# Seven products of half blocks for eleven pairs of feature tiles, and a squared relu on ScalarE alone

## The chip, the cores and the metric

One core of a Trainium2 chip runs the whole program. The metric is device time in microseconds. A matrix product runs on TensorE (PE in the profile, its weight loads PEld), elementwise work on VectorE (DVE), ScalarE (ACT) and GpSimd (POOL); SyncE (SP) issues the transfers from DRAM.

## The reference

The program computes two blocks of a sequence model in a row, on 512 tokens of width 1024, in float32. The first has a gated linear recurrence, a pooling branch and an attention to a memory, the second a spatial gating, a gated linear attention and a feed-forward part. The change lies in the feed-forward part, at the end of the second block:

```python
h = layer_norm(DEEPNORM_ALPHA * h + m @ w_out[l], ln1_g[l], ln1_b[l])     # 512 x 1024
f = jnp.square(jax.nn.relu(h @ w_ff1[l])) @ w_ff2[l]                      # 1024 -> 4096 -> 1024
h = layer_norm(DEEPNORM_ALPHA * h + f, ln2_g[l], ln2_b[l])
```

## The kernel before, in words

**Products.** Every float32 operand is split into a high part, rounded to the format fp32r, and a low part, the rest: a copy by ScalarE (`split`, L558) and a subtraction by VectorE. A product of two 128-row blocks is then three matmuls into the same accumulator (`mm3`, L575): high x high, high x low, low x high. Activations lie feature-major: a page (`pg`, 64 of them, 128 x 512) holds 128 features of all 512 tokens. PSUM has eight banks of 128 x 512.

**Weights.** They come in chunks of 512 KB, in one fixed order (`chunks`, L599). `load_to` has SP load a chunk into one of four raw buffers (tag wr); `split_to` splits it into one of four slots for the high parts (tag wh) and one of four for the low parts (wl), at an offset of columns that `shift` gives for some chunks (16 for the key projection of the memory). Chunks named in `paged` are split into pages instead. `chunk` hands out the next one.

**The stage.** After the layer norm `ln1`, `h1h` and `h1l` hold the split activations in eight pages each, and `ha` the unsplit ones. The first product (1024 -> 4096) makes 32 tiles of 128 features. Tiles 0 to 3 are one group (L1924 to L1955), with all tokens of half HA (0 to 255) first and then HB, because the norm of HB is still being computed. Tiles 4 to 31 are units (`unit_fm`, L1984): one chunk, 8 k-blocks times three matmuls of 512 columns into one bank, then ScalarE's relu out of PSUM and VectorE's product of relu and PSUM, into a page of `ff`. The second product (4096 -> 1024) then uses all eight banks; its tokens stand on the partitions, so the residual needs `ha` in tokens: `to_tokens` (L1964) transposes three of the four token tiles on TensorE, as a side lane that runs between the units, and the fourth is added in PSUM by a product of `ha` with the scaled identity `idl` (L2013).

**Order.** Nothing runs as it is called. `Recorder` (L168) records every operation; `order` (L324) lays out the whole program with a list schedule over PE, ACT, DVE, POOL and SP: each operation has a modelled cost, a priority (the latest start, worked back from the end) and the tiles it needs a free buffer for. The best of six rounds is issued, so each engine has one fixed queue. All instructions are issued from one line (L500), so the profile is read by the names of the tiles: ps is PSUM, wh and wl the weight slots, wr the raw weights, pg the pages, ct the constants.

Of the kernel before, what the change touches and what calls it, by code (L numbers as in the profile page):

```python
# [8 lines left out]
F32 = mybir.dt.float32  # L9
F32R = mybir.dt.float32r  # L10
U32 = mybir.dt.uint32
ACTF = mybir.ActivationFunctionType
ALU = mybir.AluOpType
# [7 lines left out]
ISQ = 128.0 ** -0.5  # L21

SLOT = 1088


VECS = [
# [141 lines left out]
class Recorder:  # L168
# [335 lines left out]
ORDER1 = [(w[:-1], int(w[-1])) for w in (  # L504
    "o0 o1 o2 o3 q0 k0 qc0 km0 km1 km2 km3 q1 k1 vm0 vm1 vm2 vm3 qc1 q2 k2 "
    "q3 qc3 qc2 k3 u0 u1 u2 u3 zb0 zb1 zb2 zb3 za0 za1 za2 za3 zc0 zc1 zc2 zc3").split()]
ORDER2 = [(w[:-1], int(w[-1])) for w in (
    "au0 au1 au2 au3 au4 au5 au6 au7 q0 k0 q1 r0 k1 q2 k2 q3 k3 r1 r2 r3 "
    "r4 r5 r6 r7 ga0 ga1 ga2 ga5 ga3 ga4 ga6 ga7 gb0 gb1 gb2 gb3 gb4 gb5 gb6 gb7").split()]
# [3 lines left out]
def tile_two_blocks(ctx, tc, wa, wb, xT, memT, vec, cst, rows, poolw, wst, wg2, out):  # L513
    ctx.enter_context(tc.manual_schedule())
    rec = Recorder(tc.nc)
    V, A, G, PE, SP = [Engine_(rec, e) for e in ("DVE", "ACT", "POOL", "PE", "SP")]

    per = ctx.enter_context(tc.tile_pool(name="per", bufs=1))
    sb = ctx.enter_context(tc.tile_pool(name="sb", bufs=1))
# [4 lines left out]
    def name(p):  # L524
        cnt[0] += 1
        return f"{p}{cnt[0]}"

    def pg(n=T, dt=F32):
        return rec.tile(sb, [128, n], dt, tag="pg", name=name("pg"), bufs=NPG)

    def big(n=2 * T):
        return rec.tile(sb, [128, n], F32, tag="big", name=name("big"), bufs=4)

    def bank():
        return rec.tile(psum, [128, T], F32, tag="ps", bufs=8, name=name("ps"))
# [7 lines left out]
    def tt(eng, out, a, b, op):  # L543
        eng.tensor_tensor(out=out, in0=a, in1=b, op=op)
# [10 lines left out]
    def act(out, in_, func, **kw):  # L555
        A.activation(out=out, in_=in_, func=func, **kw)

    def split(hi, lo, src, scale=None, eng=None):  # L558

        if scale is None:  # L560
            act(hi, src, ACTF.Copy)
            tt(eng or V, lo, src, f(hi), ALU.subtract)
        else:
            act(hi, src, ACTF.Copy, scale=scale)
            stt(lo, src, scale, f(hi), ALU.mult, ALU.subtract)

    def split_pg(src, n=T, **kw):
        hi, lo = pg(n, F32R), pg(n, F32R)
        split(hi, lo, src, **kw)
        return hi, lo  # L570

    def mm(out, l, r, start, stop):
        PE.matmul(out=out, lhsT=l, rhs=r, start=start, stop=stop)

    def mm3(out, lh, ll, rh, rl, start, stop):  # L575
        mm(out, lh, rh, start, False)
        mm(out, lh, rl, False, False)
        mm(out, ll, rh, False, stop)
# [30 lines left out]
            nb += 1  # L609
    RAW, HL = 4, 4  # L610
    raw, wsp, paged = {}, {}, set()

    shift = {4 + i: 16 for i, w in enumerate(ORDER1) if w[0] == "km"}
    shift.update({4 + len(ORDER1) + 12 + i: 48 for i in range(8)})
    shift[4 + len(ORDER1) + 12 + 16 + len(ORDER2) + 4] = 16
    n_ld, n_sp, look = [0], [0], [2]
# [10 lines left out]
    def load_to(i):  # L627
        while n_ld[0] <= min(i, NCH - 1):
            c = n_ld[0]
            t = rec.tile(sb, [128, src[c].shape[1]], F32, tag="wr", name=f"wr{c}", bufs=RAW)  # L630
            SP.dma_start(out=t, in_=src[c])
            raw[c] = t
            n_ld[0] += 1

    def split_to(i):
        while n_sp[0] <= min(i, NCH - 1):
            c = n_sp[0]
            t = raw.pop(c)
            n = src[c].shape[1]
            if c in paged:  # L640
                h, l = Pair(), Pair()
                for i in range(2):
                    split(h.pages[i], l.pages[i], t[:, i * T:(i + 1) * T])
            else:
                o = shift.get(c, 0)
                h = rec.tile(sb, [128, SLOT], F32R, tag="wh", name=f"wh{c}", bufs=HL)[:, o:o + n]
                l = rec.tile(sb, [128, SLOT], F32R, tag="wl", name=f"wl{c}", bufs=HL)[:, o:o + n]
                split(h, l, t)
            wsp[c] = (h, l)
            n_sp[0] += 1  # L650
# [5 lines left out]
    def lane(quick=False):  # L656
        q = deque()
        lanes.append(q)
        if quick:
            fast.append(q)  # L660
        return q
# [20 lines left out]
    ci = [0]  # L682
# [8 lines left out]
    def run_ahead():  # L691
        c = ci[0] - 1 + look[0]
        while n_sp[0] <= min(c, NCH - 1):
            load_to(n_sp[0])
            split_to(n_sp[0])
            load_to(n_sp[0] - 1 + RAW)

    def unit(emit, evac=None, early=False):
        first = True
        for _ in emit(*chunk()):  # L700
            if first:
                run_ahead()
                first = False
            step(fast)
        if early and evac:
            evac()
        step(lanes)
        if not early and evac:
            evac()

    def fm(ps, ah, al, n=T):
        def emit(wh, wl):
            for k in range(8):
                s = slice(k * 128, (k + 1) * 128)
                mm3(ps[:, 0:n], wh[:, s], wl[:, s], ah[k], al[k], k == 0, k == 7)
                if k == 3:
                    yield
        return emit

    def unit_fm(ah, al, evac, n=T):  # L720
        ps = bank()
        unit(fm(ps, ah, al, n), lambda: evac(ps))

    def units_tok(ah, al, ncol, evac, k_first=False, late=False):

# [83 lines left out]
    xh, xl = [], []  # L809
    first = []  # L810
    if True:
# [14 lines left out]
        for k in range(8):  # L826
            s = slice((k % 4) * 260, (k % 4 + 1) * 260)
# [9 lines left out]
        for k in range(8):  # L837
            s = slice((k % 4) * 260, (k % 4 + 1) * 260)
            w = first[k // 4]
            h, l = split_pg(xraw[k], scale=vc("norm_g", k))  # L840
# [61 lines left out]
    for c in range(2):  # L902
        def evac(j, ps, c=c):
            s = slice(c * 256, c * 256 + 256)
            split(vh[j][:, s], vl[j][:, s], ps[:, 0:256], scale=rxc[:, j:j + 1])
            stt(gt[:, c, j, :], ps[:, 256:260], rxc[:, j:j + 1], rsm[:, 4 * c:4 * c + 4], ALU.mult, ALU.add)
# [73 lines left out]
    mh, ml = [], []  # L980
# [784 lines left out]
    ha = []  # L1765
# [34 lines left out]
    s1 = [None]  # L1800
# [18 lines left out]
    s2 = pg()  # L1819
# [22 lines left out]
    h1h = [pg(T, F32R) for _ in range(8)]  # L1842
    h1l = [pg(T, F32R) for _ in range(8)]
# [36 lines left out]
    ps = col_sum(s1[0], 4)  # L1880
# [7 lines left out]
    p = bank()  # L1888
# [35 lines left out]
    ff = [None] * 32  # L1924
    ps_f = [bank() for _ in range(4)]
    g2 = ln1(HB)
    plan = {(0, 0): "ge", (0, 1): "gG", (1, 0): "gG", (1, 1): "g", (2, 0): "gG", (2, 1): "gG", (3, 0): "gG", (3, 1): "gG"}
    for hf in (HA, HB):
        for u in range(4):
            if hf is HA:  # L1930
                W.append(chunk())
            for kk in range(2):
                k = 2 * u + kk
                for m in range(4):
                    s = slice(kk * 512 + m * 128, kk * 512 + (m + 1) * 128)
                    mm3(ps_f[m][:, hf], W[u][0][:, s], W[u][1][:, s], h1h[k][:, hf], h1l[k][:, hf], k == 0, k == 7)
                if hf is HA:
                    for c in plan[u, kk]:
                        if c == "g":
                            next(g, None)  # L1940
                        elif c == "G":
                            next(g2)
                        else:
                            evac_half(3, HB)
                    if kk == 0 and u < 3:
                        run_ahead()
                else:
                    next(g2, None)
                    if u == 3 and kk == 0:
                        run_ahead()  # L1950
        for m in range(4):
            if hf is HA:
                ff[m] = pg()
            act(ff[m][:, hf], ps_f[m][:, hf], ACTF.Relu)
            tt(V, ff[m][:, hf], ps_f[m][:, hf], ff[m][:, hf], ALU.mult)  # L1955
    W.clear()
    del s1, s2, sq, ps_f, ps_h


    idl = pg()[:, 0:128]  # L1960
    ts(idl, ident, ALPHA, None, ALU.mult)
    ht = [[pg() for _ in range(2)] for _ in range(3)]

    def to_tokens():  # L1964
        yield
        for j in range(3):
            for c in range(2):
                p = bank()
                for i in range(4):
                    PE.transpose(out=p[:, i * 128:(i + 1) * 128], in_=ha[4 * c + i][:, j * 128:(j + 1) * 128], identity=ident)  # L1970
                act(ht[j][c], p, ACTF.Copy, scale=ALPHA)
                yield

    tl = lane()
    tl.append(to_tokens())
    def evac_f(i):
        def e(ps):
            t = pg()
            act(t, ps, ACTF.Relu)
            tt(V, t, ps, t, ALU.mult)  # L1980
            ff[i] = t
        return e

    for i in range(4, 32):  # L1984
        unit_fm(h1h, h1l, evac_f(i))
    drain_side()
    del h1h, h1l
# [24 lines left out]

    for c in range(2):  # L2013
        for i in range(4):
            mm(po[3][c][:, i * 128:(i + 1) * 128], ha[4 * c + i][:, 384:512], idl, i == 0, False)
    ha.clear()
    del idl

    split_f(0)
    split_f(1)  # L2020
# [191 lines left out]
```

## Time and profile before

| | |
|---|---|
| runs, median (lowest to highest) | 1135.74 us (1134.62 to 1136.75) |
| profiled execution | 1136.61 us |
| its span, first to last instruction | 1134.7 us |
| granted TensorE clock, mean | 0.993 of 2.4 GHz |
| PE busy | 1117.9 us, 99%, 5808 matmuls |
| DVE busy | 710.1 us, 63% |
| ACT busy | 515.8 us, 45% |
| POOL busy | 183.6 us, 16% |
| chain that ended last | PE 98%, DVE 1% |

A row of the timeline gives the start and the length of a run of equal instructions, and in brackets how long the engine had been idle and what ended that. A matmul's length in the trace overlaps the next one's, so its price is read from the distance of starts. A row of the windows gives busy time and number of instructions of each engine in a stretch, the granted clock and the share and rate of the DMA.

### The profile page before, as it was taken

The numbers are of one execution on the slowest core, as the hardware profiler recorded it, in microseconds if no ns is written. First come the engines' busy times: TensorE is split into PE (matmuls) and PEld (weight loads), VectorE is DVE, ScalarE is ACT, GpSimd is POOL, SyncE is SP. The second block draws the span as 40 slices with busy tenths as digits, with TensorE's granted clock in tenths as the row PEclk, the third lists the DMA queues.
The fourth block names the chain that finished last, engine by engine and source line by source line (L and its number), as shares of the span: only waits on it lengthen the run. The fifth ranks groups of instructions, "written<-read, shape, count | busy, mean of one in ns | idle before, by whom it ended". The sixth has DMA issues, their size and how long they took to land.

```text
span 1134.7 us, 15224 instructions
## 1 busy us (share of the span) xinstructions
PE 1117.9 (99%) x5808; PEld 954.4 (84%) x5808; DVE 710.1 (63%) x1291; ACT 515.8 (45%) x868; POOL 183.6 (16%) x244
## 2 busy tenths in 40 slices
PE   8999999999999999999999999999999999999997
PEld 8888888878889999788888887888888888888885
DVE  6978887887436565568768867986333337333324
ACT  7766536444334533874565534546332326222311
POOL 5212102000101000344145560002000000000005
PEclk9999999999999999899999999999999999999999
DMA  8324222422232322222221131431223223234201
GB/s 306 113 94 168 84 75 84 142 101 97 90 111 87 103 75 75 75 95 73 75 93 57 56 112 42 144 113 37 72 83 106 93 93 111 93 120 140 75 1 74
DMA packets 33799, 108.85 MB, mean 96 GB/s; under 512 B 3888, under 2 KB 5040, under 8 KB 33728
## 3 DMA queue, kind: packets, MB, share of 16 engines
q1 hardware_dynamic: 33728, 107.90, 28.4%
q8 instruction: 45, 0.74, 0.3%
q14 instruction: 26, 0.21, 0.1%
HBM read 105.79 MB, written 2.10 MB: 95 GB/s over the span
## 4 chain that ended last, share of the span: by engine, by line
PE 98%; DVE 1%; ACT 0%; DMA 0%; issue 0%; SPq 0%
PE ps L500 98%; DVE pg L500 0%; DMA wr<-in_wb_dram 0%; ACT pg L500 0%; DVE sm L500 0%; ACT wh L500 0%; DVE wl L500 0%; SPq L500 0%; ACT bhl L500 0%
## 5 line engine op out<-in xcount | busy, mean ns | idle before, releaser
L500 PE MATMUL ps<-pg,wh 128*128 128x512 f32 (+1 forms) x1952 | 597.0, 388 | 0.0
L500 PEld LDWEIGHTS ps<-pg,wh 128*128 128x128 f32 x1952 | 361.7, 189 | 73.5 <-PE ps L500 1.0
L500 PE MATMUL ps<-pg,wl 128*128 128x512 f32 (+1 forms) x976 | 375.7, 385 | 0.0
L500 ACT ACTIVATE wh<-wr 128x1024 fp32r<-128x1024 f32 (+2 forms) x159 | 163.1, 1026 | 322.4 <-PE ps L500 291.7
L500 DVE TENSOR_TENSOR wl<-wr,wh 128x1024 fp32r<-128x1024 f32 (+1 forms) x151 | 188.8, 1252 | 161.3 <-ACT wh L500 161.0
L500 PE MATMUL ps<-pg,pg 128*128 128x512 f32 (+4 forms) x1280 | 239.4, 343 | 1.4 <-ACT pg L500 1.4
L500 PEld LDWEIGHTS ps<-pg,pg 128*128 128x128 f32 (+1 forms) x1280 | 206.0, 191 | 30.8 <-ACT pg L500 2.3
L500 PEld LDWEIGHTS ps<-pg,wl 128*128 128x128 f32 x976 | 183.8, 188 | 37.0
L500 POOL TENSOR_TENSOR pg<-pg,pg 128x128 f32<-128x128 f32 (+4 forms) x113 | 109.5, 976 | 650.2 <-ACT pg L500 466.0
L500 ACT ACTIVATE pg<-pg 128x512 fp32r<-128x512 f32 (+6 forms) x254 | 133.4, 550 | 100.4 <-DVE pg L500 91.1
L500 PE MATMUL ps<-wh,pg 128*128 128x260 f32 (+2 forms) x800 | 169.0, 307 | 5.5 <-ACT wh L500 5.5
L500 DVE TENSOR_TENSOR pg<-ps,pg 128x512 f32<-128x512 f32 (+4 forms) x153 | 95.3, 630 | 77.2 <-PE ps L500 68.3
L500 DVE TENSOR_TENSOR pg<-pg,pg 128x512 f32<-128x512 f32 (+7 forms) x207 | 122.5, 616 | 30.3 <-PE ps L500 13.9
L500 PEld LDWEIGHTS ps<-wh,pg 128*128 128x128 f32 x800 | 130.6, 191 | 12.3 <-ACT wh L500 5.5
L500 PE MATMUL ps<-wl,pg 128*128 128x260 f32 (+2 forms) x400 | 121.4, 305 | 0.0
L500 PEld LDWEIGHTS ps<-wl,pg 128*128 128x128 f32 x400 | 76.4, 191 | 3.6 <-issue 0.5
L500 DVE TENSOR_TENSOR pg<-wr,pg 128x512 fp32r<-128x512 f32 x62 | 40.8, 689 | 61.3 <-issue 41.5
L500 ACT ACTIVATE pg<-wr 128x512 fp32r<-128x512 f32 x62 | 35.4, 624 | 83.6 <-PE ps L500 75.2
L500 DVE SCALAR_TENSOR_TENSOR pg<-pg,pg 128x512 f32<-128x512 f32 (+4 forms) x76 | 54.8, 739 | 4.5 <-ACT pg L500 4.0
L500 ACT ACTIVATE pg<-ps 128x512 f32<-128x512 f32 (+5 forms) x78 | 39.7, 529 | 12.7 <-PE ps L500 12.2
L500 ACT ACTIVATE pg<-pg,vt 128x512 f32<-128x512 f32 (+3 forms) x60 | 38.9, 656 | 13.5 <-DVE pg L500 12.1
L500 DVE SCALAR_TENSOR_TENSOR pg<-pg,vt,pg 128x512 fp32r<-128x512 f32 (+4 forms) x48 | 37.5, 793 | 6.3 <-ACT pg L500 5.4
(131 smaller groups left out, 540.6 us busy)
## 6 DMA issues: line engine op xcount, KB each, us to landing
wr<-in_wa_dram SPq DMA_DIRECT2D x172, 512.0 KB, 3.4
wr<-in_wb_dram SPq DMA_DIRECT2D x10, 520.0 KB, 3.6
pg<-in_xT_dram SPq DMA_DIRECT2D x16, 256.0 KB, 4.1
pg<-in_rows_dram SPq DMA_DIRECT2D x10, 256.0 KB, 4.2
out_dram<-pg SPq DMA_DIRECT2D x8, 256.0 KB, 2.0
wr<-in_wb_dram SPq DMA_DIRECT2D x8, 130.0 KB, 4.0
pg<-in_memT_dram SPq DMA_DIRECT2D x4, 256.0 KB, 7.1
pg<-in_wst_dram SPq DMA_DIRECT2D x2, 256.0 KB, 4.4
```

Source lines behind the costliest of these rows:

```text
L500: getattr(real[o.eng], o.what)(**kw)
```

## The change

Tiles 4 to 25, eleven pairs, are computed by a scheme of seven block products (Strassen and Winograd's). A pair's weights are a 2 x 2 array of blocks: two tiles (the raw chunks a and c) by two halves of the contraction (lo: k-blocks 0 to 3, hi: 4 to 7). The activations are a 2 x 2 array too: the same two halves of k by two halves of the tokens. `pair_weights` builds four weight slots from a, c, s1 = c.lo + c.hi, s2 = s1 - a.lo, a.lo - c.lo and a.hi - s2, with VectorE and into `big` buffers or in place. `fast_operands` builds the differences of the activation blocks once, for all pairs. `pair_fast` runs the seven products, each over four k-blocks at 256 columns, into halves of four banks, and recombines them with five VectorE instructions and a copy by ScalarE. The chunks of the pairs are skipped by `split_to`. The relu's square is taken by ScalarE, in the first group and in the units left (26 to 31) too. The transposes to tokens are recorded as a whole ahead of the pairs, and the fourth token tile of `ha` is copied into two pages (`hr`).

```diff
+NFAST = 11
...
+    FF1 = 4 + len(ORDER1) + 12 + 16 + len(ORDER2) + 8
+    fast_ff = set(range(FF1 + 4, FF1 + 4 + 2 * NFAST))
...
     def split_to(i):
         while n_sp[0] <= min(i, NCH - 1):
             c = n_sp[0]
+            if c in fast_ff:
+                n_sp[0] += 1
+                continue
...
+    def pair_weights():
+        i = ci[0]
+        ci[0] += 2
+        load_to(i + 1)
+        split_to(i + 1)
+        a, c = raw.pop(i), raw.pop(i + 1)
+        lo, hi = slice(0, 512), slice(512, 1024)
+        def slot():
+            h = rec.tile(sb, [128, SLOT], F32R, tag="wh", name=name("fh"), bufs=HL)[:, 16:16 + 1024]
+            l = rec.tile(sb, [128, SLOT], F32R, tag="wl", name=name("fl"), bufs=HL)[:, 16:16 + 1024]
+            return h, l
+        def part(w, s):
+            return w[0][:, s], w[1][:, s]
+        w1 = slot()
+        split(*w1, a)
+        s1, s2 = big(768)[:, 0:512], big(768)[:, 0:512]
+        tt(V, s1, c[:, lo], c[:, hi], ALU.add)
+        tt(V, s2, s1, a[:, lo], ALU.subtract)
+        tt(V, c[:, lo], a[:, lo], c[:, lo], ALU.subtract)
+        w2 = slot()
+        split(*part(w2, lo), s2)
+        split(*part(w2, hi), s1)
+        w3 = slot()
+        split(*w3, c)
+        tt(V, a[:, hi], a[:, hi], s2, ALU.subtract)
+        w4 = slot()
+        split(*part(w4, lo), a[:, hi])
+        load_to(i + 3)
+        return w1, w2, w3, w4
+
+    def pair_fast(b, evac, w=None):
+        w1, w2, w3, w4 = w or pair_weights()
+        lo, hi = slice(0, 512), slice(512, 1024)
+        p16, p23, p7, p45 = [bank() for _ in range(4)]
+        L, R = slice(0, 256), slice(256, 512)
+        def product(o, w, s, m):
+            wh, wl = w[0][:, s], w[1][:, s]
+            for kk in range(4):
+                q = slice(kk * 128, (kk + 1) * 128)
+                mm3(o, wh[:, q], wl[:, q], b[m][0][kk], b[m][1][kk], kk == 0, kk == 3)
+        product(p16[:, L], w1, lo, 1)
+        product(p16[:, R], w2, lo, 6)
+        product(p7[:, L], w3, lo, 7)
+        product(p45[:, R], w2, hi, 5)
+        product(p23[:, L], w1, hi, 2)
+        product(p45[:, L], w3, hi, 4)
+        product(p23[:, R], w4, lo, 3)
+        c1, c2, u = pg(), pg(), big(768)
+        act(c1[:, L], p16[:, L], ACTF.Copy)
+        tt(V, u[:, L], p16[:, R], c1[:, L], ALU.add)
+        tt(V, u[:, R], p7[:, L], u[:, L], ALU.add)
+        tt(V, c1[:, R], p45[:, R], u[:, L], ALU.add)
+        tt(V, c1, p23, c1, ALU.add)
+        tt(V, c2.rearrange("p (a n) -> p a n", a=2), p45.rearrange("p (a n) -> p a n", a=2),
+           u[:, R].unsqueeze(1).to_broadcast([128, 2, 256]), ALU.add)
+        evac(c1, c2)
+
+    def fast_operands(x, xh, xl):
+        L, R = slice(0, 256), slice(256, 512)
+        b = {m: ([None] * 4, [None] * 4) for m in range(1, 8)}
+        for kk in range(4):
+            j = kk + 4
+            for m, (t, s) in {1: (kk, L), 2: (j, L), 3: (j, R)}.items():
+                b[m][0][kk], b[m][1][kk] = xh[t][:, s], xl[t][:, s]
+            t56, t74 = pg(), pg()
+            tt(V, t56[:, L], x[kk][:, R], x[kk][:, L], ALU.subtract)
+            tt(V, t56[:, R], x[j][:, R], t56[:, L], ALU.subtract)
+            tt(V, t74[:, L], x[j][:, R], x[kk][:, R], ALU.subtract)
+            tt(V, t74[:, R], x[j][:, L], t56[:, R], ALU.subtract)
+            for (ml, mr), t in (((5, 6), t56), ((7, 4), t74)):
+                h, l = split_pg(t)
+                for m, s in ((ml, L), (mr, R)):
+                    b[m][0][kk], b[m][1][kk] = h[:, s], l[:, s]
+        return b
...
                     if u == 3 and kk == 0:
-                        run_ahead()
+                        w = pair_weights()
         for m in range(4):
             if hf is HA:
                 ff[m] = pg()
             act(ff[m][:, hf], ps_f[m][:, hf], ACTF.Relu)
-            tt(V, ff[m][:, hf], ps_f[m][:, hf], ff[m][:, hf], ALU.mult)
+            act(ff[m][:, hf], ff[m][:, hf], ACTF.Square)
...
-    tl = lane()
-    tl.append(to_tokens())
+    fb = fast_operands(ha, h1h, h1l)
+    for i in range(8):
+        act(hr[i // 4][:, (i % 4) * 128:(i % 4 + 1) * 128], ha[i][:, 384:512], ACTF.Copy)
+    for _ in to_tokens():
+        pass
+    ha.clear()
+
     def evac_f(i):
         def e(ps):
             t = pg()
             act(t, ps, ACTF.Relu)
-            tt(V, t, ps, t, ALU.mult)
+            act(t, t, ACTF.Square)
             ff[i] = t
         return e
 
-    for i in range(4, 32):
+    def evac_pair(i):
+        def e(*cs):
+            for k, t in enumerate(cs):
+                act(t, t, ACTF.Relu)
+                act(t, t, ACTF.Square)
+                ff[i + k] = t
+        return e
+
+    for i in range(4, 4 + 2 * NFAST, 2):
+        pair_fast(fb, evac_pair(i), w)
+        w = None
+    fb.clear()
+    for i in range(4 + 2 * NFAST, 32):
         unit_fm(h1h, h1l, evac_f(i))
...
-            mm(po[3][c][:, i * 128:(i + 1) * 128], ha[4 * c + i][:, 384:512], idl, i == 0, False)
+            mm(po[3][c][:, i * 128:(i + 1) * 128], hr[c][:, i * 128:(i + 1) * 128], idl, i == 0, False)
```

## Rows read from the trace of the kernel before

**Rows 1.** The page's engine totals: busy us, share of the span, instructions.
```profile
PE 1117.9 (99%) x5808; PEld 954.4 (84%) x5808; DVE 710.1 (63%) x1291; ACT 515.8 (45%) x868; POOL 183.6 (16%) x244
```

**Rows 2.** The chain that ended last, in order of time: start, length, what.
```profile
785.35 340.96 PE ps L500 x1548
```

**Rows 3.** Windows: length, busy us (instructions) by engine, clock, DMA share, GB/s.
```profile
764.00:786.00 22.00, 19.11 (x146) 17.72 (x146) 17.59 (x51) 14.02 (x32) 3.94 (x5) 0.98 0.15 48
786.00:790.30 4.30, 4.30 (x27) 4.25 (x27) 3.74 (x10) 3.65 (x9) 1.47 (x2) 0.70 0.01 4
790.30:795.40 5.10, 5.10 (x45) 5.10 (x44) 0.02 (x1) 0.78 (x3) 0.73 (x1) 1.00 0.00 0
...
802.00:857.00 55.00, 55.00 (x253) 45.54 (x252) 18.27 (x20) 16.94 (x25) 0.00 (x0) 1.00 0.28 93
```

**Rows 4.** Timeline, ScalarE in two units: start, length, operation, idle before.
```profile
801.06 1.06 ACT L500 ACTIVATE wh<-wr 128x1024 fp32r<-128x1024 f32 x1 [4.63 <-PE ps L500]
...
802.02 0.58 ACT L500 ACTIVATE pg<-ps 128x512 f32<-128x512 f32 x1
...
806.50 1.06 ACT L500 ACTIVATE wh<-wr 128x1024 fp32r<-128x1024 f32 x1 [3.89 <-PE ps L500]
```

**Rows 5.** Timeline, TensorE in the key projection of the memory.
```profile
82.06 0.28 PE L500 MATMUL ps<-pg,wl 128*128 128x256 f32 x1
...
84.10 0.28 PE L500 MATMUL ps<-pg,wl 128*128 128x256 f32 x1
```

**Rows 6.** Timeline, TensorE in the out projection at half width.
```profile
734.37 0.28 PE L500 MATMUL ps<-pg,wl 128*128 128x256 f32 x1
...
735.78 0.28 PE L500 MATMUL ps<-pg,wl 128*128 128x256 f32 x1
```

**Rows 7.** Timeline, TensorE in the first feed-forward group, half HB.
```profile
789.14 6.87 PE L500 MATMUL ps<-pg,pg 128*128 128x256 f32 x56
...
795.84 0.40 PE L500 MATMUL ps<-pg,wh 128*128 128x512 f32 x1
```

**Rows 8.** Groups by form, 700 to 1000 us: count, busy us, mean ns, idle before.
```profile
L500 DVE TENSOR_TENSOR wl<-wr,wh 128x1024 fp32r<-128x1024 f32 x41 | 50.1, 1225 | 102.3 <-ACT wh L500 102.2
...
L500 DVE TENSOR_TENSOR pg<-ps,pg 128x256 f32<-128x256 f32 x16 | 6.6, 424 | 10.3 <-ACT pg L500 5.4 <-PE ps L500 4.9
...
L500 DVE TENSOR_TENSOR pg<-pg,pg 128x512 f32<-128x512 f32 x9 | 6.2, 689 | 0.3
```

**Rows 9.** Timeline, runs of equal instructions on VectorE and ScalarE.
```profile
723.98 2.36 DVE L500 TENSOR_TENSOR wl<-wr,wh 128x1024 fp32r<-128x1024 f32 x2
...
764.55 1.99 DVE L500 TENSOR_TENSOR pg<-pg,ps 128x256 f32<-128x256 f32 x5
...
954.38 3.70 DVE L500 TENSOR_TENSOR pg<-pg,pg 128x512 fp32r<-128x512 f32 x6
...
958.66 3.83 ACT L500 ACTIVATE pg<-pg 128x512 fp32r<-128x512 f32 x7
```

**Rows 10.** The page's DMA issues: count, KB each, us to landing.
```profile
wr<-in_wa_dram SPq DMA_DIRECT2D x172, 512.0 KB, 3.4
```

**Rows 11.** Timeline, four transposes to tokens between two units.
```profile
811.97 0.60 PE L500 MATMUL ps<-ct,pg 128*128 128x128 f32 x4
```

**Rows 12.** Timeline, TensorE at the first of three equal stops.
```profile
783.16 0.62 PE L500 MATMUL ps<-pg,pg 128*128 128x256 f32 x3 [0.47 <-ACT pg L500]
```

**Rows 13.** Windows behind these stops; the third last number is the granted clock.
```profile
785.00:786.00 1.00, 0.65 (x3) 0.65 (x4) 0.14 (x2) 0.97 (x3) 0.00 (x0) 0.58 0.00 0
786.00:787.00 1.00, 1.00 (x6) 1.00 (x6) 1.00 (x3) 0.47 (x2) 0.69 (x1) 0.50 0.00 0
787.00:788.00 1.00, 1.00 (x6) 1.00 (x6) 0.97 (x4) 0.97 (x3) 0.04 (x1) 0.50 0.06 16
788.00:789.00 1.00, 1.00 (x8) 1.00 (x7) 0.97 (x4) 0.97 (x3) 0.17 (x1) 0.71 0.00 0
```

More of the change, by code (lines that the diff above doesn't have):

```diff
@@ L1954, in tile_two_blocks @@
             act(ff[m][:, hf], ps_f[m][:, hf], ACTF.Relu)
-            tt(V, ff[m][:, hf], ps_f[m][:, hf], ff[m][:, hf], ALU.mult)
+            act(ff[m][:, hf], ff[m][:, hf], ACTF.Square)
     W.clear()
     del s1, s2, sq, ps_f, ps_h
-    idl = pg()[:, 0:128]
+    idl = rec.tile(per, [128, 128], F32, name="idl")
+    hr = [pg(), pg()]
     ts(idl, ident, ALPHA, None, ALU.mult)
@@ L2014, in tile_two_blocks @@
         for i in range(4):
-            mm(po[3][c][:, i * 128:(i + 1) * 128], ha[4 * c + i][:, 384:512], idl, i == 0, False)
-    ha.clear()
-    del idl
+            mm(po[3][c][:, i * 128:(i + 1) * 128], hr[c][:, i * 128:(i + 1) * 128], idl, i == 0, False)
+    del idl, hr
     split_f(0)
```

## The prediction

> **What bounds the kernel now.** The page's engine totals come first: TensorE is busy for 1117.9 of 1134.7 us, VectorE for 63% [rows 1]. The chain of waits says that this busy time is also the path: from 785.35 us on it is one piece of TensorE work, 340.96 us long, that reaches into the last evictions [rows 2]. The windows by stage show the other engines around the change: while tiles 4 to 14 of the first feed-forward product run (802 to 857), VectorE works 18.27 of 55 us and ScalarE 16.94 [rows 3]. So in this stage a column less on TensorE is time, as long as no other engine becomes the limit. The question is whether VectorE, at a third before, stays behind TensorE when it also has to build the sums of blocks.
>
> **TensorE: what goes and what comes.** A pair of tiles took 2 x 24 matmuls of 512 columns. One unit is the distance of two weight splits on ScalarE, 801.06 to 806.50, 5.44 us [rows 4], so 226.7 ns a matmul and 10.88 us a pair. The pair now takes seven products of 4 k-blocks by 3 matmuls (high x high, high x low, low x high): 84 matmuls of 256 columns, 12.5% fewer columns. Their price is bounded by three rows. The key projection of the memory has the same form (weights in a wh slot shifted by 16 columns, halves of pages streaming): 18 matmuls from 82.06 to 84.10, 113.3 ns [rows 5]. The out projection at half width, also with weights in a wh slot: 12 from 734.37 to 735.78, 117.5 ns [rows 6]. The first group of feed-forward tiles, with weights in pages: 56 from 789.14 to 795.84, 119.6 ns [rows 7]. The last is the upper bound (10.05 us a pair), the first the lower (9.52). The new weights lie in slots, so I take the middle of the two rows with slots, 115.5 ns: 9.70 us a pair. That removes 1.18 us a pair, 13.0 us for eleven (bounds 9.1 and 15.0).
>
> **VectorE and ScalarE within a pair.** VectorE gets: two splits of 1024, three of 512, four sums or differences of 512 (s1, s2, the low half of c, the high half of a), three evictions of 256 and two of 512. By the durations of single instructions (1225, 689 and 424 ns, the splits of 512 costed as the sums [rows 8]) that is 2 x 1.225 + 9 x 0.689 + 3 x 0.424 = 9.92 us, more than TensorE's 9.70. By the pitch of instructions that follow each other it is less: six of 512 in 3.70 us are (3.70 - 0.69)/5 = 0.60 each, two of 1024 in 2.36 are 1.13, five of 256 in 1.99 are 0.39 [rows 9]; 2 x 1.13 + 9 x 0.60 + 3 x 0.39 = 8.83 us. I take the pitch, because VectorE will have something queued nearly always: 91% of the pair. Before, a pair cost it 2 x (1.13 + 0.60) = 3.5 us.
> The Trainium skill ("VectorE: DVE Perf Modes", section "The DRAIN you can't avoid") says that the next VectorE instruction does not start until the pipe of the one before has emptied; by whole durations in a row VectorE would be the limit at 9.92 us or more a pair, and the sum would lose at least 0.22 x 11 = 2.4 us. The trace disagrees in size: 0.60 us from one start to the next against a duration of 0.69 [rows 8, 9].
> ScalarE gets two copies of 1024 (0.96 us from one start to the next [rows 4]), three of 512, a copy of 256 and two relus and two squares of 512: with 0.53 us for a 512 (seven in 3.83 us [rows 9]) some 1.9 + 1.6 + 0.4 + 2.1 = 6.0 of 9.70 us. That is no limit. The square's move takes 0.60 us from VectorE and adds 0.53 to ScalarE for a tile, both idle two thirds of the stage before [rows 3]; I cost it at nothing, and without that cover it would be half a microsecond on ScalarE per tile.
>
> **The waits in a pair.** There are four weight slots, and a pair fills all. With 1.39 us a product, the slot of w2 falls free after the fourth product (5.5 us), that of w1 after the fifth (6.9), w3 after the sixth (8.3), w4 at the end (9.7). The next pair's w1 takes the first: 0.96 us of copy and 1.13 of subtraction, ready at about 7.7 of the 9.7 us when nothing stands ahead of it. Its w2 is wanted at 11.1, its w3 at 12.5. Behind w1 on VectorE's queue stand the two halves of w2 (1.2), two full evictions (1.2) and w3 (1.13): they end at 11.2, 1.3 before w3 is wanted. So the cycle closes, with 1 to 2 us to spare, if the order on VectorE is near this one. For queueing in another order I add 0.15 us a pair, 1.7 us in all (bounds 0 and 1.13 a pair: one split of 1024 that stands ahead of the wrong instruction). The transfers do not decide: 1 MB a pair, each chunk 3.4 us from issue to landing [rows 10], with raw buffers freed early in each pair. SP issues the same number of them.
>
> **Getting into the first pair.** Added VectorE work ahead of it: the moving operands, 16 differences of 256 and 8 splits of 512, 16 x 0.39 + 8 x 0.60 = 11.0 us, and the first pair's weights, 2 x 1.13 + 7 x 0.60 = 6.5 us; 17.5 together. VectorE's idle time up to 795.4 is 4.4 + 0.6 + 5.1 = 10.1 us [rows 3]; a full weight split (1.13) and four squares (1.6) leave it, so 12.8 us fit and 4.7 are left over at 795.8, when the first group ends. TensorE can meanwhile run products 1 and 2 of the first pair, which need only h1 and w1 (24 x 115.5 ns = 2.8 us), and the 24 transposes to tokens, which are now recorded ahead of the pairs (four in 0.60 us [rows 11], together 2.7 with what they wait): 5.5 us of cover for 4.7. The cover is not used in full, since the last operands of h1 exist only at about 790; I take a stall of 2.0 us. It is at worst the 4.7 and some handovers, 6 us. Below nothing: in the first group itself TensorE stands 0.47 us three times for a relu, and then runs at a granted clock of 0.50, 1.2 instead of 2.4 GHz, for some 3 us [rows 12, 13]; a new order there could give back up to 3 us. The eight copies of 128 columns for the last token tile and the six transposed tiles go to ScalarE, which is busy for 0.78 of 5.1 us there [rows 3].
>
> **Sum.** 13.0 - 1.7 - 2.0 = 9.3 us less. The profiled execution took 1136.61 us (1134.7 of span and 1.9 around it), so 1127.3; it is 0.87 above the median of the runs, 1135.74, so about 1126.5 as a median.
>
> **Rivals.**
> First, VectorE becomes the limit. For it: 9.92 us by durations, several dependent instructions in a row (s1, s2, then the difference with s2), and a copy by ScalarE ahead of each split. Against it: the pitch [rows 9]. With 0.4 us of such handovers on top of the durations, 10.3 us a pair, the gain is 0.58 x 11 = 6.4, less 3 for a longer start: 3.4 us, 1132.4.
> Second, the other side: the slot cycle does not close. If the order on the queues puts the next pair's w1 behind the last evictions of the present one, its copy and subtraction (0.96 + 1.13 = 2.1 us) lie bare on TensorE's path in each pair: 9.70 + 2.1 = 11.8 us, 0.92 more than before, 10 us over eleven pairs and 2 at the start: 1147.5. The point from which it decides is 1.0 us of bare time a pair (13.0 less the start, over eleven). Repeated stops may also bring 1.2 GHz, as the three in the first group did [rows 12, 13]. For it: four slots, all taken by one pair. Against it: w2's slot is free 4.2 us before the pair ends.
> Third, the change does what it says but its matmuls run at 119.6 ns and the start costs 6 us: 9.1 - 1.7 - 6 = 1.4 us, no change that can be told.
>
> **Numbers.** Forecast 0.60 (its own range 1119 to 1130.5: 113.3 ns with little stall, to 119.6 ns with 3 us of start); VectorE the limit 0.20; slots 0.15; no change 0.05. What a measurement can tell from no change is about 0.2%, 1133.5 to 1138. Of the second case a fifth falls into that. So faster 0.76, same 0.09, slower 0.15. The range 1119 to 1138 leaves out the slots' case and a little below 1119, where the stops of the first group would vanish as well.
>
> **What would show it.** Right: 5808 + 11 x 36 = 6204 matmuls on the page; in the eleven pairs a period of 9.6 to 10.1 us, matmuls of 256 columns 113 to 120 ns apart; VectorE 85 to 95% busy there with TensorE never waiting over 0.3 us a pair; one stall of about 2 us just before product 6 or 7 of the first pair, released by VectorE. Wrong: TensorE idle in every pair, released by the low halves of weights (the slots) or by VectorE's differences (the limit); a granted clock under 1 within the pairs; or a 256-column price above 120 ns, which would take the forecast's main term.

## The result, and the profile after

The changed kernel took 1119.51 us (median of four runs, 1119.03 to 1120.66) against 1136.24 us of the kernel before: ratio 0.9857, 95% interval 0.9845 to 0.987, that is 15 to 18 us less. The profiled execution took 1119.03 us with a span of 1117.3. The forecast was 1126.5; the direction and the mechanism held, the size was 16.7 us instead of 9.3. One run of the kernel before, beside the last group of experiments, took 2275.6 us and enters no figure here.

The page of the changed kernel, engine totals (to be held against [rows 1]):
```profile
PE 1100.6 (99%) x6204; PEld 958.1 (86%) x6204; DVE 771.1 (69%) x1411; ACT 564.2 (50%) x964; POOL 182.7 (16%) x244
```
There are 6204 matmuls, 396 more, and TensorE is still busy for 99%: more instructions, fewer columns, the same bound.

Windows of the changed kernel, columns as in [rows 3]: the first pair, the second, the third to fifth, the sixth, the last five.
```profile
792.00:802.65 10.65, 10.34 (x85) 9.89 (x85) 9.53 (x20) 10.30 (x21) 0.00 (x0) 1.00 0.19 68
802.65:815.05 12.40, 11.89 (x102) 11.50 (x101) 11.19 (x17) 6.89 (x11) 0.00 (x0) 1.00 0.27 87
815.05:843.61 28.56, 28.56 (x254) 28.56 (x253) 26.53 (x42) 19.48 (x30) 0.00 (x0) 1.00 0.37 112
843.61:854.13 10.52, 10.00 (x86) 9.80 (x85) 8.95 (x15) 6.49 (x11) 0.00 (x0) 1.00 0.35 100
854.13:901.70 47.57, 47.57 (x422) 47.57 (x421) 44.63 (x70) 33.63 (x54) 0.00 (x0) 1.00 0.35 116
```
Three pairs in 28.56 and five in 47.57 us are 9.52 and 9.51 us a pair with TensorE never idle; VectorE works 26.53 / 3 = 8.84 us of each, 93%, ScalarE 68%. Only the first, second and sixth pair are longer: by 1.1, 2.9 and 1.0 us. In the second, 1.8 us are not a stop: sixteen matmuls with the scaled identity, which stood behind the last unit before, were placed there (first two rows below). The sixth stops for an eviction of 256 columns (last row).

Timeline of TensorE in the changed kernel:
```profile
803.11 0.60 PE L502 MATMUL ps<-idl,pg 128*128 128x128 f32 x4
...
803.79 1.50 PE L502 MATMUL ps<-idl,pg 128*128 128x128 f32 x12
...
851.40 0.39 PE L502 MATMUL ps<-pg,fh 128*128 128x256 f32 x1 [0.52 <-DVE pg L502]
```
So eleven pairs lose 1.1 + 1.1 + 1.0, some 3.1 us, around three stops. TensorE is idle for 1.3 us of that (0.31, 0.51 and 0.52, length less busy time in the windows); the rest goes to matmuls that run dearer next to a stop. Two other stretches differ. In the first group the three stops of [rows 12] are gone: 60 matmuls run through, and transposes to tokens fill the place where half HA ends.
```profile
774.71 7.85 PE L502 MATMUL ps<-pg,pg 128*128 128x256 f32 x60
782.40 1.47 PE L502 MATMUL ps<-ct,pg 128*128 128x128 f32 x12
```
The 3.4 us at 1.2 GHz that stood behind those stops [rows 13] are not gone: a stretch as long now stands 22 us earlier, behind a stop of 0.81 us at the group's start, where the kernel before ran at the full clock. TensorE's row there, and windows behind it:
```profile
762.28 0.44 PE L502 MATMUL ps<-ct,pg 128*128 128x128 f32 x2 [0.81 <-ACT pg L502]
...
763.00:764.00 1.00, 1.00 (x7) 1.00 (x7) 1.00 (x4) 0.97 (x3) 0.31 (x1) 0.52 0.00 0
764.00:766.00 2.00, 2.00 (x11) 2.00 (x11) 1.96 (x6) 1.74 (x5) 0.49 (x2) 0.50 0.00 0
```
And around 455 us, 300 us ahead of anything the change touches, the clock of the kernel before had fallen, of which the prediction had no row. Windows of the kernel before there (the third last number is the granted clock):
```profile
453.00:454.00 1.00, 1.00 (x6) 0.78 (x5) 1.00 (x2) 0.81 (x2) 0.00 (x0) 1.00 0.00 0
454.00:455.00 1.00, 1.00 (x4) 0.49 (x2) 1.00 (x3) 0.92 (x2) 0.00 (x0) 0.54 0.00 0
455.00:456.00 1.00, 1.00 (x3) 0.65 (x3) 0.47 (x1) 0.50 (x1) 0.00 (x0) 0.50 0.00 0
456.00:458.00 2.00, 2.00 (x7) 1.52 (x6) 1.20 (x2) 1.98 (x3) 0.00 (x0) 0.50 0.00 0
```
The same windows of the changed kernel:
```profile
454.00:455.00 1.00, 1.00 (x5) 0.58 (x4) 1.00 (x2) 0.65 (x1) 0.00 (x0) 1.00 0.00 0
455.00:456.00 1.00, 1.00 (x6) 0.81 (x5) 0.18 (x1) 0.78 (x2) 0.00 (x0) 1.00 0.00 0
456.00:458.00 2.00, 2.00 (x11) 1.65 (x10) 1.48 (x2) 1.97 (x3) 0.00 (x0) 1.00 0.03 8
```
In both TensorE was at the same twelve matmuls of 16 rows; first the kernel before, then the changed one:
```profile
451.76 3.56 PE L500 MATMUL ps<-pg,pg 16*128 16x512 f32 x12
```
```profile
451.48 3.03 PE L502 MATMUL ps<-pg,pg 16*128 16x512 f32 x12
```
From 454.1 us on the one ran at 1.2 instead of 2.4 GHz for 6.8 us, the other did not. Matmul by matmul the changed kernel is 0.28 us ahead up to this place and 3.46 us ahead after it: 3.2 us of the 17.4 between the two spans.

### The profile page after: what moved, and what is told of

The parts are those of the page before. It is cut to its first block, busy times and chain, and to the rows that moved or that the text cites. A ratio compares the mean times of both kernels' runs of the same rounds, so it can differ in the third digit from the quotient of the medians.

```text
span 1117.3 us, 16271 instructions
## 1 busy us (share of the span) xinstructions
PE 1100.6 (99%) x6204; PEld 958.1 (86%) x6204; DVE 771.1 (69%) x1411; ACT 564.2 (50%) x964; POOL 182.7 (16%) x244
## 4 chain that ended last, share of the span: by engine, by line
PE 96%; ACT 2%; DVE 1%; DMA 0%; issue 0%; SPq 0%; DVEq 0%
PE ps L502 96%; ACT pg L502 1%; DVE pg L502 1%; DVE wl L502 0%; DMA pg<-in_xT_dram 0%; ACT wh L502 0%; DVE sm L502 0%; SPq L502 0%; DVE sel L502 0%; DVE selc L502 0%; DVEq L502 0%
## 5 line engine op out<-in xcount | busy, mean ns | idle before, releaser
L502 PE MATMUL ps<-pg,wh 128*128 128x512 f32 (+1 forms) x1600 | 485.7, 386 | 0.0
L502 PEld LDWEIGHTS ps<-pg,wh 128*128 128x128 f32 x1600 | 294.4, 188 | 59.4 <-PE ps L502 0.7
L502 PE MATMUL ps<-pg,wl 128*128 128x512 f32 (+1 forms) x800 | 305.9, 383 | 0.0
L502 PE MATMUL ps<-pg,pg 128*128 128x512 f32 (+3 forms) x1264 | 236.5, 343 | 0.1
L502 ACT ACTIVATE pg<-pg 128x512 f32<-128x512 f32 (+7 forms) x328 | 174.2, 554 | 110.7 <-DVE pg L502 100.3
L502 PEld LDWEIGHTS ps<-pg,pg 128*128 128x128 f32 x1264 | 203.8, 191 | 28.8 <-ACT pg L502 0.6
L502 DVE TENSOR_TENSOR pg<-pg,pg 128x512 fp32r<-128x512 f32 (+7 forms) x227 | 130.8, 603 | 23.1 <-ACT pg L502 14.9
L502 PE MATMUL ps<-pg,fh 128*128 128x256 f32 x616 | 105.4, 277 | 0.8 <-DVE pg L502 0.8
L502 PEld LDWEIGHTS ps<-pg,fh 128*128 128x128 f32 x616 | 91.8, 188 | 1.7 <-DVE pg L502 1.2
L502 PE MATMUL ps<-pg,fl 128*128 128x256 f32 x308 | 81.6, 277 | 0.5 <-ACT pg L502 0.5
```

The costliest lines, as they stand in the source:

```text
L502: getattr(real[o.eng], o.what)(**kw)
```

## The experiments

The runs of a group were timed on one chip beside the kernel before, whose median was 1136.28 us (20 runs), 1136.91 (13) and 1135.73 (7) in the three groups.

**The change without its products.**
```diff
-NFAST = 11
+NFAST = 0
-                        w = pair_weights()
+                        run_ahead()
-    fb = fast_operands(ha, h1h, h1l)
+    fb = {}
```


> The rest of the change without the seven products: all 28 units as before, squares on ScalarE, transposes recorded ahead, the copies for the last token tile. Theory (the gain is the columns: 11 x 1.36 = 15.0 us, less 3.1 us of stops in three pairs): this gives back 12 us and more, 1132 to 1136, within 0.4% of the kernel before. Rival (the new order of the whole program and the moved square bring a good part, since the two profiles already differ by 3.5 us ahead of the feed-forward part): 1126 to 1131.


Measured: 1131.57 us (1131.28 to 1133.46), ratio 0.9961 (0.9949 to 0.9973). It lies between the two forecasts: 4.7 us of the gain do not come from the products. Against the profile of the kernel before, 2.8 us of them are there by 759 us, as this one ran at the full clock at 455 us; some 1.9 come after. The products alone are worth 1131.57 - 1119.51 = 12.1 us. That is what the windows above give: eleven pairs at 10.88 - 9.52 = 1.36 us are 15.0, less 3.1 around the stops, 11.9.

**The first group's square back on VectorE**, in that kernel:
```diff
-            act(ff[m][:, hf], ff[m][:, hf], ACTF.Square)
+            tt(V, ff[m][:, hf], ps_f[m][:, hf], ff[m][:, hf], ALU.mult)
```


> The first experiment with one thing put back: in the first group of four tiles the square is VectorE's product of relu and PSUM again. Theory (the three stops of 0.47 us and the half clock behind them came from the bank being read twice): the stops return, 1132.5 to 1134. Rival (they went with the new order around the transposes): 1131 to 1132.


Measured: 1134.75 us (1132.73 to 1136.58), ratio 0.999 (0.9979 to 1.0). The stops came back as they were. Timeline of TensorE in this kernel:
```profile
781.65 0.62 PE L502 MATMUL ps<-pg,pg 128*128 128x256 f32 x3 [0.47 <-ACT pg L502]
782.74 0.62 PE L502 MATMUL ps<-pg,pg 128*128 128x256 f32 x3 [0.47 <-ACT pg L502]
783.83 3.70 PE L502 MATMUL ps<-pg,pg 128*128 128x256 f32 x17 [0.47 <-ACT pg L502]
```
and with them a stretch at 1.2 GHz from 783.6 us on. The kernel without this edit has one stop of 0.47 there, and its stretch at 1.2 GHz, of the same 3.4 us, at 764.4 us. The median lies above the forecast, 3.2 us above that of the kernel without the edit. But the profile of the kernel with the edit also ran at 1.2 GHz for 3.4 us at 456 us, which the edit does not touch: that costs 1.6 us ahead of the group. From there on the two profiles differ by 1.6 us, and the fastest runs by 1.5. So the square of the first group's eight half tiles is worth about 1.5 us, by the stops and not by the clock. It is the edit together with the order that the planner makes of it; the two were not taken apart.

**All squares back on VectorE, products kept.**
```diff
-            act(t, t, ACTF.Square)
+            tt(V, t, ps, t, ALU.mult)
...
-                act(t, t, ACTF.Square)
+                tt(V, t, t, t, ALU.mult)
```
(and in the first group, as above)


> The seven products stay, every square goes back to VectorE (the pairs' as a product in SBUF). Theory (VectorE has 8.84 us of work in a pair of 9.52 and two squares of 0.60 make it 10.04): VectorE becomes the limit, a pair takes 10.0 to 10.3 us, 1125 to 1128. Rival (the square is a side matter, as the prediction costed it): pairs of 9.52 and 1119 to 1121.


Measured: 1132.84 us (1129.87 to 1136.06), ratio 0.9977 (0.9961 to 0.9993): most of the gain is gone, more than either forecast said, and the eleven pairs take 123.4 us instead of 109.7 (3.4 us of that in the second pair at 1.2 GHz, behind its stops). Windows of this kernel over eight pairs:
```profile
821.40:907.00 85.60, 83.12 (x673) 79.55 (x672) 80.05 (x129) 41.74 (x64) 0.00 (x0) 1.00 0.32 98
```
10.7 us a pair, VectorE at 94%. Its work is 10.0 us a pair, as expected, and the pair takes 0.7 more than that: VectorE is the limit and still waits for TensorE once in each pair, and TensorE in each pair for the copy into a slot (0.2 us) and for the split behind it (0.1). VectorE as the limit does not mean VectorE at 100%.

**One sum of 512 more on VectorE.**
```diff
         tt(V, s1, c[:, lo], c[:, hi], ALU.add)
+        tt(V, s1, c[:, lo], c[:, hi], ALU.add)
```


> One sum of 512 columns (s1) is done twice in each pair, so VectorE has 0.60 us more. Theory (VectorE is priced by the distance of starts: 8.84 + 0.60 = 9.44 of 9.52): pairs stay at 9.5 to 9.7 us, 1119.5 to 1122. Rival (VectorE pays whole durations, 9.92 before and 10.6 now, and was hidden by slack that is used up): pairs of 10.1 to 10.6, 1126 to 1131.


Measured: 1131.38 us (1128.76 to 1133.66), ratio 0.9958 (0.9945 to 0.9972). The theory missed: 0.60 us that should have fitted into 9.52 made pairs of 10.3 to 10.8. Waits in this kernel over the pairs (who waited for whom, us in total, times, longest):
```profile
ACT pg L502 <- DVE pg L502: 31.7, 10, 3.9
...
DVE big L502 <- PE ps L502: 5.1, 9, 0.8
PEld ps L502 <- ACT pg L502: 3.4, 5, 0.7
PEld ps L502 <- ACT fh L502: 2.9, 8, 0.5
```
From the third pair on TensorE stops once in each pair, in turn for two things: in five pairs for ScalarE's copy of 256 columns out of PSUM (0.47 to 0.53 us), in four for ScalarE's copy into a weight slot (0.30). One stop of each kind, and the rows of ScalarE and VectorE ahead of the second:
```profile
844.22 0.38 PE L502 MATMUL ps<-pg,fl 128*128 128x256 f32 x1 [0.53 <-ACT pg L502]
...
852.06 1.02 PE L502 MATMUL ps<-pg,fh 128*128 128x256 f32 x4 [0.30 <-ACT fh L502]
...
849.00 2.48 ACT L502 ACTIVATE pg<-pg 128x512 f32<-128x512 f32 x4 [3.88 <-DVE pg L502]
851.39 1.13 ACT L502 ACTIVATE fh<-big 128x512 fp32r<-128x512 f32 x2
...
848.28 0.68 DVE L502 TENSOR_TENSOR pg<-ps,big 128x512 f32<-128x512 f32 x1
849.08 0.69 DVE L502 TENSOR_TENSOR pg<-ps,pg 128x512 f32<-128x512 f32 x1
849.69 0.68 DVE L502 TENSOR_TENSOR big<-wr 128x512 f32<-128x512 f32 x1
850.40 0.69 DVE L502 TENSOR_TENSOR big<-big,wr 128x512 f32<-128x512 f32 x1
```
The last row is s2. It starts 2.12 us after the first full eviction: the planner has put the second eviction ahead of it, and the added sum. In the changed kernel it is 0.60:
```profile
881.65 0.68 DVE L502 TENSOR_TENSOR pg<-ps,big 128x512 f32<-128x512 f32 x1
882.25 0.68 DVE L502 TENSOR_TENSOR big<-big,wr 128x512 f32<-128x512 f32 x1
```
Yet in the kernel with one more, s2 is done at 851.09, and ScalarE copies it only at 851.39, when its relus and squares of the pair before are through. So VectorE was not simply full: the sum came with another order on the queues, and VectorE still waits for TensorE in each pair (5.1 us in nine waits). Whether 0.60 us would fit into the old order is not shown.

**Where the weights lie.** The slots start at column 0, or 48, instead of 16.
```diff
-            h = rec.tile(sb, [128, SLOT], F32R, tag="wh", name=name("fh"), bufs=HL)[:, 16:16 + 1024]
+            h = rec.tile(sb, [128, SLOT], F32R, tag="wh", name=name("fh"), bufs=HL)[:, 0:1024]
```
(the low half alike; in the second kernel 48:48 + 1024)


> The pairs' weight slots start at column 0 instead of 16. Theory (the 113.3 ns a matmul come from where the weights lie against the slot's start): 117.5 to 119.6 ns, pairs of 9.87 to 10.05 us, 1123.5 to 1125.5. Rival (weights in a slot stream at 113.3 ns whatever the offset): pairs of 9.52, 1119 to 1121.

> The pairs' weight slots start at column 48 instead of 16 (at 0 a pair took 10.08 us, at 16 it takes 9.52 or 9.89). Theory (the offset against the page that streams sets the price, and 0 alone is bad): 113.3 or 117.7 ns, 1119 to 1122. Rival (only 16 is good): 120 ns, pairs of 10.08, 1123.5 to 1125.5.


Column 0: 1124.65 us (1123.69 to 1125.08), ratio 0.9897 (0.988 to 0.9914); eight pairs without a stop take 10.08 us, a matmul 120 ns. Column 48: 1124.72 us (1122.89 to 1125.75), ratio 0.9904 (0.9881 to 0.9928); the third to fifth pair take 9.52 and the last five 9.89; within the sixth the price rises to 117.7 ns some 4 us ahead of its stop. Its total missed the forecast of 1119 to 1122 although its pairs met it, since its profile has the 6.8 us at 1.2 GHz at 455 us again. So of the three offsets 0 is dear, and 16 and 48 give 113.3 or 117.7 ns.

**The changed kernel once more.**


> The changed kernel once more, beside the others. Both theories: 1119 to 1121. What it tells is whether its times have one level, where those of the kernel before have two (1133.1 to 1133.9 and 1135.9 to 1137.4).


Measured: 1120.56 us (1119.65 to 1123.67), ratio 0.9864 (0.9844 to 0.9884). It has no one level: the price of a matmul in this profile is not that of the first. Timeline of TensorE in it, in the last pairs, one low-weight matmul in three:
```profile
880.68 0.28 PE L502 MATMUL ps<-pg,fl 128*128 128x256 f32 x1
...
881.04 0.28 PE L502 MATMUL ps<-pg,fl 128*128 128x256 f32 x1
```
The same in the first profile of the changed kernel:
```profile
880.20 0.28 PE L502 MATMUL ps<-pg,fl 128*128 128x256 f32 x1
...
880.54 0.28 PE L502 MATMUL ps<-pg,fl 128*128 128x256 f32 x1
...
880.88 0.28 PE L502 MATMUL ps<-pg,fl 128*128 128x256 f32 x1
```
0.34 us for three matmuls there, 113.3 ns; here 0.36, and over whole pairs 9.89 us, 117.7 ns. Here the switch comes at the stop in the sixth pair, and five pairs then cost 1.9 us more, with the same program. In the first profile the price had risen to 117.7 within that pair and fell back to 113.3 at the stop. What sets it was not found.

**Relieving VectorE, and another order.** s1 on GpSimd, or the planner's VectorE costs set to the measured distance of starts:
```diff
-        tt(V, s1, c[:, lo], c[:, hi], ALU.add)
+        tt(G, s1, c[:, lo], c[:, hi], ALU.add)
```
```diff
-            o.cost = 140 + 1.045 * n + 65 * ptr
+            o.cost, o.tail = 68 + 1.04 * n + 65 * ptr, 130
```


> The sum s1 of each pair goes from VectorE to GpSimd, which does nothing in this stage; a 512 takes it 1.30 us. Theory (the 3.1 us of stops in pairs 0, 1 and 5 come from VectorE being at 93%; with 0.60 us less it is at 87%): most of the stops go, 1117 to 1119. Rival (the stops come from the order that the planner fixed, or GpSimd and VectorE hold each other up at SBUF): 1119.5 to 1123.

> The kernel after with the planner's cost of a VectorE instruction set to the measured distance of starts (68 + 1.04 n ns, 600 for 512 columns, where it has 675), its tail to 130 ns. Nothing computed differs, only the order on the queues. Theory (the planner takes VectorE for the limit, 9.7 us a pair against 9.66, and orders accordingly): pairs of 9.52 without the stop in the sixth, 1117.5 to 1119.5. Rival (the order is as good either way): 1119 to 1121. A new order elsewhere can add some us.


GpSimd: 1126.32 us (1123.04 to 1128.21), ratio 0.9903 (0.9877 to 0.9928). True costs: 1125.79 us (1124.34 to 1126.03), ratio 0.9902 (0.9887 to 0.9917). Both theories fell: more stops, not fewer. With true costs nothing computed differs, yet eight of the pairs take 10.3 us: the new order makes TensorE stand some 0.5 us in each for ScalarE's copy out of PSUM, and about 0.8 are lost with the dearer matmuls behind it. With GpSimd there are six stops for three (its profile has the 6.8 us at 455 us as well), and VectorE's splits of s1 and s2 became longer. That group in the kernel with GpSimd, and in the changed kernel:
```profile
L502 DVE TENSOR_TENSOR fl<-big,fh 128x512 fp32r<-128x512 f32 x18 | 14.9, 835 | 0.0
```
```profile
L502 DVE TENSOR_TENSOR fl<-big,fh 128x512 fp32r<-128x512 f32 x18 | 11.6, 688 | 0.1
```
147 ns on average. Seven of the 18 took 975 to 1394 ns, each while GpSimd was at a sum; four more that ran beside one kept their length, as did the other seven (675 to 682). What VectorE was spared, it partly paid back beside GpSimd.

**An ordinary unit ahead of the pairs.**
```diff
-    NPG = 64
+    NPG = 65
-    fast_ff = set(range(FF1 + 4, FF1 + 4 + 2 * NFAST))
+    fast_ff = set(range(FF1 + 5, FF1 + 5 + 2 * NFAST))
-    for i in range(4, 4 + 2 * NFAST, 2):
-        pair_fast(fb, evac_pair(i), w)
+    unit_fm(h1h, h1l, evac_f(4))
+    for i in range(5, 5 + 2 * NFAST, 2):
+        pair_fast(fb, evac_pair(i))
```
(the first pair's weights are recorded with the pair, the units left begin at 27; in the second kernel ten pairs, 64 pages, and units from 25)


> One ordinary unit (tile 4) stands between the first group and the eleven pairs (tiles 5 to 26), with one page more (65). Theory (the stops in the first two pairs, 1.1 and 1.0 us, come from the 17.5 us of VectorE work ahead of the first pair, and a unit of 5.44 us of TensorE that asks VectorE for 1.13 us hides 4 us of it): the first two pairs near 9.52 us, 1117 to 1119 when the rest of the order stays. Rival (each order that the planner finds has stops of its own, as the two kernels with another order had): 1119.5 to 1126.

> As the kernel with one ordinary unit ahead, with ten pairs and the 64 pages of before. Theory: one pair less costs 1.36 us, the stops of the first two pairs go (2.1 us): 1118 to 1120.5. Rival (stops of its own): 1121 to 1127.


Eleven pairs: 1116.36 us (1116.33 to 1118.35), ratio 0.9836 (0.9817 to 0.9854). Windows of this kernel, first pair and the last nine:
```profile
796.93:809.20 12.27, 11.80 (x101) 11.59 (x100) 9.48 (x16) 8.93 (x16) 0.00 (x0) 1.00 0.25 87
...
818.72:904.41 85.69, 85.69 (x759) 85.69 (x757) 79.41 (x125) 61.01 (x94) 0.00 (x0) 1.00 0.38 118
```
The first pair has the sixteen identity matmuls in it and 0.9 us lost around one stop; all others take 9.52. It is the fastest kernel of the study, faster than its own forecast of 1117 to 1119: its slowest run, 1118.35, is below the fastest of the eight of the changed kernel, 1119.03, though the intervals against the kernel before overlap. Not all of it comes from the pairs: its profile has no stretch at 1.2 GHz at 763 us, and from 758 us to the end of the first group it takes 1.0 us less than the changed kernel; what follows takes 2.4 us less. Ten pairs: 1119.08 us (1117.58 to 1120.71), ratio 0.9856 (0.9836 to 0.9876): a pair less for the stops gone, no gain, as expected.

## Why the prediction was right, and where its size was off

**What bounds it: right.** TensorE stays the limit in the pairs, VectorE right behind. The forecast of VectorE's work by the distance of starts, 8.83 us a pair, met 8.84 (8.93 in the last five pairs). Whole durations (the first rival, 9.92) did not come about. The Trainium skill ("VectorE: DVE Perf Modes", section "The DRAIN you can't avoid") says that the next instruction does not start until the pipe is empty, but also that one that is not held starts earlier. The prediction cited the first half alone; the trace agrees with the second: 0.60 us from start to start against a duration of 0.69.

**The columns: term too small, 13.0 for 15.0.** I took the middle of two rows with weights in slots. The row of the same form and the same offset of 16 [rows 5] was the better one: 113.3 ns. But the other value was not wrong either: 117.7 ns is a second level that the same program has in some executions. With it in five pairs the term is 13.1.

**Stops: 3.7 forecast, 3.1 measured**, 2.1 at the start for 2.0 and 1.0 in the pairs for 1.7. The total is right, the place only in part, and that is some luck. The forecast was one stall of 2 us ahead of product 6 or 7 of the first pair, released by VectorE. There came 0.31 us in the first pair, released by VectorE, and 0.47 in the second, released by ScalarE's copy out of PSUM, each with dearer matmuls next to it. A unit put ahead of the first pair takes most of this away, but a stop of the second kind stays.

**The square: its price was right, its weight was not seen.** Costing the move at nothing was right for ScalarE, which is busy 68% in the pairs. But I held it against the stage before, where VectorE is idle for two thirds. In the pairs VectorE has 0.7 us left and two squares are 1.2: put back, they cost 13.7 us within the pairs. The sum for VectorE, 8.83, rests on the move, and the prediction did not say so. Nor is the rest up to 100% simply free. VectorE's 91% (93% measured) fitted the order of the changed kernel; with one sum more the order that the planner found did not hide it. How much of that is the sum and how much the order is open: the kernel with true costs lost 0.8 us in eight of its pairs by an order alone.

**The first group: bounded, but valued at zero.** The prediction named up to 3 us that a new order could give back, the three stops and the half clock behind them. 1.5 to 2 came back, about what the stops cost; the half clock only moved, to 763 us.

**The clock at 455 us: not seen.** The sum started from one profiled execution, and that one had 6.8 us at 1.2 GHz that cost 3.2. In the first group of experiments seven of the 20 runs of the kernel before took 1133.1 to 1133.9 us, at a mean granted clock of 0.996 or 0.997, and 13 took 1135.9 to 1137.4, at 0.993 to 0.995. No fast one was profiled, so that the seven lack this stretch is likely and not shown. The changed kernel's two profiles had no such stretch there, nor had six of the ten other kernels; two had it for 6.8 us and two for 3.4. Against the lower level the change is worth 13.6 to 14.4 us. What decides between the two was not found: TensorE's matmuls ahead of the place are the same, at the same distances.

So 15.0 - 3.1 = 11.9 from the products, about 2 from the first group and about 3 from the clock at 455 us make the 16.7. The forecast left out both of the last and took 2.0 too little for the columns; the three misses point the same way, and 1119.51 is only half a microsecond inside the forecast's own range.

**The slot cycle** (the rival on the other side) did not stop the changed kernel. It shows where VectorE has more to do: with the squares back TensorE waits 0.3 us in each pair for a slot, with one sum more 0.30 us in every second pair, instead of the 2.1 that I priced.

## What to carry to other kernels

A rewrite that trades TensorE columns for elementwise work pays as long as the elementwise engine stays below the pair's time; two squares too many took most of the gain. Below that limit the busy share does not tell what is free: look at which wait ends last in each pair, and remember that an edit gives the planner a new order, which alone cost 0.8 us a pair here. Price such work by the distance of starts of equal instructions, and a matmul by the row with the same width, weights and offset. Before the sum, look through the whole span for stretches at the lower clock, and compare with the fastest runs too; after it, look whether a stretch that is gone in one place stands in another.

## What the runs showed of the hardware

- The price of a 256-column fp32r matmul with weights of its own has three levels, all at the full granted clock: 113.3, 117.7 and 120 ns. Weights at column 0 of a slot gave 120, at 16 and 48 the lower two. In one execution the change from 113.3 to 117.7 came at a stop of 0.5 us and stayed for 50 us, in another of the same program the price fell back to 113.3 at that stop.
- VectorE's subtractions of 512 columns beside a sum of 512 on GpSimd took 975 to 1394 ns in seven of eleven cases, and otherwise 675 to 682.
- At twelve matmuls of 16 rows the granted clock fell to 1.2 GHz, for 3.4 or 6.8 us, in five of 13 profiles and not in the others, with TensorE never idle there.
